# Four edits around the DeltaNet stages of a one-core hybrid block: one lane transpose for four, 22 weight low parts made in the feed-forward part, 128-row exponents, another stage order

## The chip, the cores and the metric

The kernel runs on one core of a Trainium2 chip. The metric is device time in microseconds (us); the median of the runs counts. A core has five engines that run on their own: TensorE (PE, matmuls; its weight loads are shown as PEld), VectorE (DVE), ScalarE (ACT), GpSimd (POOL) and SyncE (SP), which here issues every DMA. Each engine works through its own list of instructions in order; semaphores make one wait for another.

## What is computed

A block of two layers on 256 context and 256 latent tokens of width 1024. Layer 0 mixes tokens by a gated linear recurrence, layer 1 by a bidirectional gated DeltaNet with 8 key heads and 16 value heads of 128; behind each comes a SwiGLU feed-forward part of width 2816 (22 tiles of 128). Every sub-layer is normalised and modulated by six vectors that come from a product with `ada_w`. The DeltaNet of the reference, per chunk of tokens:

```
diff = gc[..., :, None] - gc[..., None, :]
decay = jnp.where(incl, jnp.exp(jnp.where(incl, diff, 0.0)), 0.0)
m = jnp.where(strict, jnp.einsum('bhid,bhjd->bhij', kb, kc) * decay, 0.0)
sol = lax.linalg.triangular_solve(m, rhs, left_side=True, lower=True, unit_diagonal=True)
u, w = sol[..., :d_v], sol[..., d_v:]
v_new = u - jnp.einsum('bhcd,bhde->bhce', w, s)
attn = jnp.where(incl, jnp.einsum('bhid,bhjd->bhij', qc, kc) * decay, 0.0)
```

All of it is float32.

## The kernel before

**Products.** A product of two float32 matrices is made from three fast matmuls (`mm3`, line 722): each operand is split into a high part, rounded to the short format `fp32r`, and a low part, the rest. For a weight tile of 128 x 1024 (`weight`, line 704) a DMA loads it as `raw`, ACT or DVE copies it to `whi`, and DVE or POOL subtracts (`wlo = raw - whi`). There are three raw buffers, and two each of `whi` and `wlo`. `product` (line 943) takes such a pair and issues 24 matmuls: 512 columns wide for keys and values and in the feed-forward part of layer 0, 256 wide for queries and the gate z.

**Background steps.** The feed-forward part of layer 0 (`ffn`, line 1099: 22 gate and up pairs, then the down products) also carries the modulation vectors of layer 1. `ada_later` queues generators, and every product takes one step of them by `bg_step`. A step (`ada_steps`, line 734) loads 128 x 1024 of `ada_w` into one of two buffers of the tile `ring`, multiplies it by a column of `cs` and adds to an accumulator.

**The DeltaNet stages.** Two key heads (four value heads) make a group; the groups are 0 to 3. The stages, each a function, are:

- A (line 1310), per key head: four products (k, two v, q), a convolution and SiLU (tile `cu`), transposes, and spills of k and v to device memory.
- E (line 1357), per group: the exponents of the decays. For each of eight pairs of chunk and direction `exponents` (line 1275) adds three matmuls in one bank: a column part (`pick` x `cT`, 64 rows deep, from `column`, line 1386), a row part (`rows` x `own`) and a mask (`below`, `identr`). ACT takes the exponential into the tile `gn`.
- N (line 1389), per group: `gn` is multiplied by the products of the keys (`ps_g`); then the 32 x 32 diagonal blocks of its 32 matrices are gathered into the tile `lw` by four DVE transposes of 32 partitions each, and inverted by 60 small DVE operations (`lmul`, `lw`). Two transposes of all 128 partitions (`ld`, `ldt`) bring them back.
- L (line 1432): the inverse is put together from the blocks by matmuls of 32 and of 64 rows (`ps_w`, `ps_z`) with copies between.
- P (line 1528): the exponents of the attention (`ps_a`, 16 groups of three matmuls; for one direction the column part is `npick` x `rT`, which is 128 rows deep) and their products with q.
- C (line 1552): the recurrence over the chunks (`ps_y`, `ps_s`, `ps_ks`, `ps_qs`, `ps_o`).
- Z and W: the gate products, and the first output products (`ps_wo`), which fill in.

**What sets the order.** Nothing is issued as written. A `Recorder` records all operations of a section and places them on the engines by priority: an operation's place in the program plus a bias of its stage. The string `PROG` sets in which order the stages are recorded, the table `TUNE['bias']` the biases, `_cost` what the planner takes an operation to last. Operations recorded through `R.copy`, `R.tt` and the like may go to either of two engines. Since all are issued by the planner, the profile puts them all down to line 612; they are told apart by the names of the tiles.

Of the kernel before, what the change touches and what calls it, by code (L numbers as in the profile page):

```python
# [21 lines left out]
NK = 8  # L22
EPS = 1e-6
FF = 22
NQK = 8
# [17 lines left out]
def _shuffle(sh, pattern, sizes):  # L43
# [18 lines left out]
    for g, n in zip(lhs, sh.shape, strict=True):  # L62
# [3 lines left out]
        for a in g:  # L66
# [5 lines left out]

PROG = "A0 A1 E0 A2 N0 A3 E1 L0 P0 N1 C0 A4 A5 E2 P1 L1 N2 C1 A6 Z0 A7 E3 L2 P2 N3 Z1 C2 Z2 Z3 L3 W0 P3 C3"
TUNE = dict(warm=5000, ev=3000, stay=(300, 0), g0=4, early=(1, 2, 4, 6), eb=0, ea=(0, 1, 1, 1), nwo=2, prog=PROG,
            bias={'C3': -1500, 'N0': 100, 'N': -700, 'Z3': -1200, 'L': -1500, 'E3': 700, 'W': 10000, 'L3': -800, 'E': -300, 'W0': 10000, 'P': -100, 'E0': -300, 'N3': -700, 'P2': 0, 'C': 400, 'A': 700, 'Z': 700, 'C1': 0})

# [122 lines left out]
class Recorder:  # L199
# [59 lines left out]
    def _cost(self, eng, method, out, ins, kw, args):  # L259
        n = out.free() if isinstance(out, _AP) else 1  # L260
        src_psum = any(i.t.psum for i in ins) or (isinstance(out, _AP) and out.t.psum)
        if eng == "PE":
            lhs, rhs = ins[0], ins[1]
            k, m, w = lhs.sh.shape[0], lhs.free(), rhs.free()
            if lhs.dt == F32R:
                return max(w / 2.4 + 13, 118)
            if method == "transpose":
                return 110 if k == 4 else 56
            if w <= 8:
                return 215  # L270
            if m <= 64:
                first = out.sh.flat[0] < out.t.sh.size // 4
                return (max(4 * w / 2.4, 54) + 2) if first or m > 32 else 27
            return max(4 * w / 2.4, 213) + 4
        if eng == "DVE":
            if method == "transpose":
                return 1.85 * n + 70
            if method == "tensor_tensor_scan":
                return 2.08 * n + 70
            if method == "reciprocal":  # L280
                return 6.4 * n + 60
            if method == "memset":
                return 0.3 * n + 40
            ptr = 65 if method in ("tensor_scalar", "scalar_tensor_tensor") and any(i.free() == 1 for i in ins) else 0
            one = method in ("tensor_scalar", "tensor_copy")
            return (0.52 if one and not src_psum else 1.04) * n + 65 + ptr
        if eng == "ACT":
            ptr = 65 * sum(1 for x in ("scale", "bias") if isinstance(kw.get(x), _AP))
            return 0.83 * max(n, ins[0].free()) + 95 + ptr
        if eng == "POOL":  # L290
            if method == "dma_start":
                return 1000
            if method == "affine_select":
                return 1.1 * n + 30
            if method == "memset":
                return 0.87 * n + 25
            if kw.get("op", args[3] if len(args) > 3 else None) == OP.pow:
                return 165 * n + 298
            return 2.25 * n + 30
        return 60  # L300
# [320 lines left out]
def hybrid_block(ctx: ExitStack, tc: tile.TileContext, I, out, dbg=None):  # L621
# [81 lines left out]

    def weight(*src, cols=1024, aside=False, place=None):

        r = raws.pop(0) if raws else raw_load(src, cols)
        hi, lo = place or (wp.tile([128, 1024], F32R, tag=t, bufs=NB[t], name=t) for t in ("whi", "wlo"))
        if aside:
            S.activation(hi[:, :cols], r[:, :cols], AF.Copy)
        else:  # L710
            R.copy(hi[:, :cols], r[:, :cols])
        (R.tt if (cur["wide"] or cur.get("flex")) and not aside else G.tensor_tensor)(lo[:, :cols], r[:, :cols], hi[:, :cols].bitcast(F32),
                                                                 OP.subtract)
        return hi, lo
# [19 lines left out]
    def ada_steps(l, m, direct=False):  # L734
# [35 lines left out]
        for t in range(2):  # L770
# [4 lines left out]
                        b.rearrange("p (g t o) -> p g t o", t=2, o=1).to_broadcast([128, 4, 2, 2]), OP.add)  # L775
        yield

    def ada_later(l, *ms, direct=False):
# [163 lines left out]

    def product(src, n_k, xs, n, wmap=lambda w, k: w[:, 128 * k:128 * k + 128]):
        wh, wl = early.pop(0) if early else weight(src)
        bg_step()
        ps = bank("mm", "ps_mm")
        for k in range(n_k):
            a, b = xs(k)
            mm3(ps[:, 0:n], wmap(wh, k), wmap(wl, k), a, b, k == 0, k == n_k - 1)
        return ps  # L950
# [148 lines left out]
    def ffn(l, n, upd, hh, hl, first=None):  # L1099
# [7 lines left out]
        for j in range(FF):  # L1107
# [3 lines left out]
            else:  # L1111
                pg = product(I["ffn_gu"][l, 0, j], NK, xk, n)
                pu = product(I["ffn_gu"][l, 1, j], NK, xk, n)
            sg = tmp(n, name="sg")
            S.activation(sg, pg[:, 0:n], AF.Silu)
# [15 lines left out]
    dump("x1", x.rearrange("p k t -> p (k t)"))  # L1131
    ada_later(1, 0, 1, 2, 3, 4, 5)

# [116 lines left out]
    V.tensor_scalar(npick, id64, -1.0, None, OP.mult)  # L1250
    pick = dn.tile([128, 32], F32R, name="pick")
    V.tensor_tensor(pick[0:64], ident[0:64, 0:32], ident[0:64, 32:64], OP.add)
    mod4 = piece(4)
# [21 lines left out]
    def exponents(g, c, d, sign, bound, col, to, name="ps_e"):  # L1275
# [3 lines left out]
        i = 4 * c + g  # L1279
        lhs, rhs, n = col  # L1280
        T.matmul(p4, lhs, rhs.rearrange("p (h o) -> p h o", o=1).to_broadcast([n, 4, 128]), start=True, stop=False, needs=to)
        T.matmul(p4, own[sign][:, i:i + 1].to_broadcast([128, 128]), rows[d], start=False, stop=False)
# [27 lines left out]
    def stage_a(h):  # L1310
        a = A[h] = {}

        ps = product(I["dn_w_in"][8 + h], NK, hx1, 512) if h else ps_k0
        kT = a["kT"] = dn.tile([128, 512], F32, tag="kT", bufs=8, name="kT")
# [17 lines left out]
        for j in range(2):  # L1332
            ps = product(I["dn_w_in"][16 + 2 * h + j], NK, hx1, 512)
            v2 = conv_silu(ps, 16 + 2 * h + j, 2)
# [22 lines left out]
    def stage_e(g):  # L1357
# [19 lines left out]
        T.transpose(pt[0:64, 0:128], cb.rearrange("p a s -> p (a s)").bitcast(F32), ident)  # L1377
        cT = t["cT"] = dn.tile([128, 128], F32R, tag="cT", bufs=2, name="cT")
        V.tensor_copy(cT[0:64], pt[0:64, 0:128])
# [6 lines left out]
    def column(t, c, d):  # L1386
        return t["cT"][0:64], pick[0:64, 4 * (2 * c + d):4 * (2 * c + d) + 4], 64

    def stage_n(g):
# [11 lines left out]
        for q in range(2):  # L1401
# [6 lines left out]
            for c in range(4):  # L1408
                for d in range(2):
                    e = g5[:, c, d, 2 * q:2 * q + 2, :]  # L1410
                    V.scalar_tensor_tensor(e, pg[:, 128 * c:128 * c + 128].rearrange("p (a i) -> p a i", a=1)
                                           .to_broadcast([128, 2, 128]), -1.0, e, OP.mult, OP.mult)

        w = dn.tile([128, 32, 32], F32, tag="lane", bufs=3, name="lw")
        for b in range(4):
            r = slice(32 * b, 32 * b + 32)
            V.transpose(w[r], gn[r, :, 32 * b:32 * b + 32].rearrange("p s f -> p f s"))
        V.memset(w.rearrange("p a b -> p (a b)")[:, 0:1024:33], 1.0)
# [109 lines left out]
    def stage_p(g):  # L1528
# [3 lines left out]
        for c in range(2):  # L1532
            for d in range(2):
                col = (rT[:, 1], npick[:, 16 * (2 + c) + 4 * g:16 * (2 + c) + 4 * g + 4], 128) if d else column(t, 2 + c, 0)
                p4 = exponents(g, 2 + c, d, 1, (1, -1)[d], col, t["at"], "ps_a")
# [298 lines left out]
```

## Time and profile before

| | us |
|---|---|
| median of three runs | 1360.35 |
| lowest and highest run | 1358.46, 1365.85 |
| profiled execution | 1364.68 |
| its span, first to last instruction | 1363.0 |

The mean granted clock of PE is 0.976 of the full one. Of the span, 262 to 610 us are the feed-forward part of layer 0, some 640 to 1130 the DeltaNet stages, and from 1157 on the feed-forward part of layer 1. In a row of a table by stage the busy time of an engine stands with the number of its instructions; a busy PE is not PE at its peak, since the ends of matmuls are modelled, and the distance from the start of one matmul to that of the next tells what one costs in a row. In rows of groups, `out<-in` are the names of the tiles, then count, busy us, mean ns, and the idle time before them with its releaser.

### The profile page before, as it was taken

How to read it: one execution, taken by the hardware profiler on the slowest of the kernel's cores; microseconds unless marked ns; L12 is line 12 of the kernel's file. 1: busy time of each engine (PE TensorE's matmuls, PEld its weight loads, DVE VectorE, ACT ScalarE, POOL GpSimd, SP SyncE). 2: the span in 40 equal slices, each digit the busy share in tenths (PEclk: the TensorE clock that was granted, in tenths of full speed). 3: DMA queues.
4: the chain of work that ended last, by engine and by line, in shares of the span. 5: the costliest groups of instructions: out<-in, count | busy, mean ns of one | idle time of the engine just before them, and what ended most of it. 6: DMA issues, size and time to landing. Idle time of an engine off the chain costs nothing.

```text
span 1363.0 us, 23260 instructions
## 1 busy us (share of the span) xinstructions
PE 1308.6 (96%) x9200; PEld 1110.3 (81%) x9200; DVE 1035.0 (76%) x1851; ACT 564.9 (41%) x1053; POOL 229.6 (17%) x203
## 2 busy tenths in 40 slices
PE   5999999899999999999998999999998998999997
PEld 3677778878888888888867788898798888999997
DVE  5799986988775665557868889798499376877775
ACT  3388773444321111005746656747646431211100
POOL 2000000110100001212524333334243100000000
PEclk9899999899999999999999999999999699999999
DMA  9545423365564665333523222323133025455563
GB/s 352 197 165 188 140 94 114 124 202 196 188 228 164 192 208 183 98 110 125 178 74 129 71 78 79 105 71 121 63 117 117 25 92 180 139 182 180 179 181 116
DMA packets 61261, 195.60 MB, mean 144 GB/s; under 512 B 6752, under 2 KB 9952, under 8 KB 60896
## 3 DMA queue, kind: packets, MB, share of 16 engines
q1 hardware_dynamic: 61152, 194.12, 42.8%
q8 instruction: 72, 1.18, 0.4%
q14 instruction: 37, 0.30, 0.1%
HBM read 184.13 MB, written 9.96 MB: 142 GB/s over the span
## 4 chain that ended last, share of the span: by engine, by line
PE 56%; issue 15%; DVE 6%; ACT 4%; DMA 1%; POOL 0%; POOLq 0%; SPq 0%; ACTq 0%; DVEq 0%
PE ps_mm L612 29%; PE ps_dn L612 9%; PE ps_e L612 2%; PE ps_wo L612 2%; PE ps_y L612 2%; PE ps_w L612 2%; PE ps_z L612 2%; PE ps_s L612 1%; DVE lw L612 1%; PE ps_ks L612 1%; DVE cu L612 1%; PE ps_a L612 1%; PE ps_qs L612 1%; PE ps_o L612 1%; ACT gn L612 1%
## 5 line engine op out<-in xcount | busy, mean ns | idle before, releaser
L612 PE MATMUL ps_mm<-hh,whi 128*128 128x512 f32 (+1 forms) x888 | 327.4, 370 | 8.0 <-DVE cu L612 5.6
L612 PE MATMUL ps_mm<-hl,whi 128*128 128x512 f32 (+1 forms) x888 | 327.3, 370 | 0.9 <-DVE hl L612 0.8
L612 PE MATMUL ps_mm<-hh,wlo 128*128 128x512 f32 (+1 forms) x888 | 326.2, 368 | 1.7 <-POOL wlo L612 1.7
L612 DVE TENSOR_TENSOR wlo<-raw,whi 128x1024 fp32r<-128x1024 f32 (+2 forms) x183 | 220.5, 1205 | 17.4 <-ACT whi L612 8.3
L612 DVE CAST whi<-raw 128x1024 fp32r<-128x1024 f32 (+2 forms) x177 | 120.2, 679 | 145.8 <-PE ps_mm L612 81.0
L612 POOL TENSOR_TENSOR wlo<-raw,whi 128x1024 fp32r<-128x1024 f32 x55 | 132.0, 2402 | 506.5 <-DVE whi L612 351.3
L612 PEld LDWEIGHTS ps_mm<-hh,whi 128*128 128x128 f32 x888 | 169.6, 191 | 40.6 <-issue 9.9
L612 PEld LDWEIGHTS ps_mm<-hh,wlo 128*128 128x128 f32 x888 | 169.7, 191 | 29.6 <-POOL wlo L612 2.4
L612 PEld LDWEIGHTS ps_mm<-hl,whi 128*128 128x128 f32 x888 | 170.0, 192 | 27.4 <-DVE hl L612 2.0
L612 PE MATMUL ps_dn<-fh,wlo 128*128 128x256 f32 (+1 forms) x374 | 122.7, 328 | 0.0
L612 PE MATMUL ps_dn<-fl,whi 128*128 128x256 f32 (+1 forms) x374 | 122.5, 327 | 0.0
L612 PE MATMUL ps_dn<-fh,whi 128*128 128x256 f32 (+1 forms) x374 | 122.2, 327 | 0.0
L612 PE MATMUL ps_mm<-h2h,whi 128*128 128x256 f32 x352 | 100.4, 286 | 1.1 <-ACT h2h L612 1.1
L612 PE MATMUL ps_mm<-h2l,whi 128*128 128x256 f32 x352 | 100.6, 286 | 0.5 <-DVE h2l L612 0.3
L612 PE MATMUL ps_mm<-h2h,wlo 128*128 128x256 f32 x352 | 100.1, 284 | 0.0
L612 ACT ACTIVATE whi<-raw 128x1024 fp32r<-128x1024 f32 (+2 forms) x61 | 63.2, 1036 | 77.8 <-PE ps_mm L612 45.1
L612 ACT ACTIVATE fh<-sg 128x256 fp32r<-128x256 f32 (+1 forms) x43 | 22.4, 522 | 156.4 <-DVE sg L612 156.3
L612 ACT ACT_TABLE_LOAD x59 | 75.7, 1283 | 7.0 <-DMA sm<-small 3.4
L612 PEld LDWEIGHTS ps_dn<-fl,whi 128*128 128x128 f32 x374 | 71.1, 190 | 6.4 <-issue 0.4
L612 PEld LDWEIGHTS ps_dn<-fh,wlo 128*128 128x128 f32 x374 | 71.1, 190 | 6.4 <-issue 0.4
L612 PEld LDWEIGHTS ps_dn<-fh,whi 128*128 128x128 f32 x374 | 71.1, 190 | 6.0
L612 DVE SCALAR_TENSOR_TENSOR x<-ring,cs,x 128x1024 f32<-128x1024 f32 x49 | 63.9, 1304 | 15.4 <-DMA ring<-ada_w 14.4
(326 smaller groups left out, 2544.7 us busy)
## 6 DMA issues: line engine op xcount, KB each, us to landing
ring<-ada_w SPq DMA_DIRECT2D x96, 512.0 KB, 4.5
raw<-ffn_gu SPq DMA_DIRECT2D x88, 512.0 KB, 3.5
raw<-dn_w_in SPq DMA_DIRECT2D x49, 512.0 KB, 3.5
raw<-ffn_down SPq DMA_DIRECT2D x34, 512.0 KB, 3.6
raw<-rg_w_in SPq DMA_DIRECT2D x16, 512.0 KB, 4.5
raw<-ffn_down SPq DMA_DIRECT2D x17, 384.0 KB, 3.4
raw<-dn_w_out SPq DMA_DIRECT2D x12, 512.0 KB, 3.6
raw<-rg_w_out SPq DMA_DIRECT2D x10, 512.0 KB, 3.4
```

Of the source, the lines that this page charges most:

```text
L612: call(*[real(x) for x in args], **{n: real(v) for n, v in kw.items()})
```

## The change

It has five parts.

1. In `exponents` the column part gets 128 rows: `cT` becomes two fixed tiles with zeros in rows 64 to 127, and `pick` is zero there.
2. In stage N, ACT copies the four diagonal blocks into a tile `lc`, and one DVE transpose of 128 partitions makes `lw`.
3. For 22 key and value weight tiles of stage A (all but that of the first key and of the first value) the low part is made in the feed-forward part of layer 0, as 22 further background steps: load into `ring`, copy on ACT, subtraction, store to device memory. Stage A then loads `wlo` by a DMA into its place. Every second pair of the feed-forward part takes one background step more.
4. `PROG` and the biases are others: A0 to A3 come first, E3 stands ahead of Z0 and L2, and P3 and L3 ahead of Z3.
5. The planner's costs of three kinds of operation are others; these change no instruction, only places.

```
-PROG = "A0 A1 E0 A2 N0 A3 E1 L0 P0 N1 C0 A4 A5 E2 P1 L1 N2 C1 A6 Z0 A7 E3 L2 P2 N3 Z1 C2 Z2 Z3 L3 W0 P3 C3"
+PROG = "A0 A1 A2 A3 E0 E1 N0 L0 P0 A4 N1 C0 P1 A5 E2 L1 N2 C1 A6 A7 E3 Z0 L2 P2 C2 Z1 N3 Z2 L3 P3 Z3 W0 C3"
...
-    def weight(*src, cols=1024, aside=False, place=None):
+    def weight(*src, cols=1024, aside=False, place=None, low=None):
...
+        if low is not None:
+            R.copy(hi, r)
+            sync.dma_start(out=lo.bitcast(F32), in_=low)
+            return hi, lo
...
+    def low_steps(tiles):
+
+        low = dr.tile([len(tiles), 128, 1024], F32, name="low")
+        for n, i in enumerate(tiles):
+            r, hi = next(cur["araw"]), cur["acc"][:, 1]
+            sync.dma_start(out=r, in_=I["dn_w_in"][i], after=cur["late"])
+            S.activation(hi.bitcast(F32R), r, AF.Copy)
+            R.tt(r.bitcast(F32R), r, hi, OP.subtract)
+            sync.dma_start(out=low[n], in_=r)
+            LOW[i] = low[n]
+            yield
...
+                bg_step(l == 0 and j % 2)
...
-    ada_later(1, 0, 1, 2, 3, 4, 5)
+    ada_later(1, 0, 1)
+    cur["bg"].append(low_steps([i for h in range(NQK) for i in (8 + h, 16 + 2 * h, 17 + 2 * h)][2:2 + TUNE["low"]]))
+    ada_later(1, 2, 3, 4, 5)
...
+    G.memset(pick.bitcast(F32), 0.0)
+    cTs = [dn.tile([128, 128], F32R, name=f"cT{i}") for i in range(2)]
+    for x in cTs:
+        G.memset(x[64:128].bitcast(F32), 0.0)
...
     def column(t, c, d):
-        return t["cT"][0:64], pick[0:64, 4 * (2 * c + d):4 * (2 * c + d) + 4], 64
+        return t["cT"], pick[:, 4 * (2 * c + d):4 * (2 * c + d) + 4]
...
+        lc = dn.tile([128, 32, 32], F32, tag="lane", bufs=3, name="lc")
         w = dn.tile([128, 32, 32], F32, tag="lane", bufs=3, name="lw")
         for b in range(4):
             r = slice(32 * b, 32 * b + 32)
-            V.transpose(w[r], gn[r, :, 32 * b:32 * b + 32].rearrange("p s f -> p f s"))
+            S.activation(lc[r], gn[r, :, 32 * b:32 * b + 32], AF.Copy)
+        V.transpose(w, lc.rearrange("p s f -> p f s"))
```

What the planner makes of it, at three places. On SP, in the feed-forward part of layer 0, near the last gate and up products: `raw` are that part's weights, `ring` the buffers of the background steps. Before:

```order
L612 DMA raw<-ffn_gu 128x1024
L612 DMA ring<-ada_w 128x1024 x2
L612 DMA raw<-ffn_gu 128x1024 x3
L612 DMA raw<-ffn_down 128x1024 x2
L612 DMA ring<-ada_w 128x1024 x2
L612 DMA raw<-ffn_down 128x768
```

And now:

```order
L612 DMA ring<-dn_w_in 128x1024
L612 DMA raw<-ffn_gu 128x1024
L612 DMA low<-ring 128x1024 x2
L612 DMA ring<-dn_w_in 128x1024
L612 DMA raw<-ffn_gu 128x1024
L612 DMA ring<-dn_w_in 128x1024
L612 DMA raw<-ffn_down 128x1024
L612 DMA low<-ring 128x1024 x2
```

Where pairs of ada loads stood between weight loads, two loads and two stores of low parts go round with two weight loads.

On SP at the start of the DeltaNet stages, with `wlo<-low` the low parts that come back. Before:

```order
L612 DMA raw<-dn_w_in 128x1024 x3
L612 DMA kspill<-k 128x512
L612 DMA raw<-dn_w_in 128x1024
L612 DMA kl<-kspill 128x512
L612 DMA raw<-dn_w_in 128x1024
```

And now:

```order
L612 DMA raw<-dn_w_in 128x1024
L612 DMA wlo<-low 128x1024
L612 DMA raw<-dn_w_in 128x1024 x3
L612 DMA kspill<-k 128x512
L612 DMA raw<-dn_w_in 128x1024
L612 DMA kl<-kspill 128x512
L612 DMA wlo<-low 128x1024
L612 DMA vspill<-vp 128x512
```

Each low part stands ahead of a weight load and waits for PE to have done with its buffer.

On DVE, around the lane transpose of group 3 (`gn` is the tile of the matrices, `lw` the gathered blocks, `lc` ACT's copy of them). Before:

```order
L612 SCALAR_TENSOR_TENSOR gn<-ps_g,gn 128x256 x16
L612 SCALAR_TENSOR_TENSOR r<-ps_ks,nbc,vl 128x128
L612 STREAM_TRANSPOSE lw<-gn 32x1024 x4
L612 SCALAR_TENSOR_TENSOR r<-ps_ks,nbc,vl 128x128
L612 MEMSET lw 128x32
L612 SCALAR_TENSOR_TENSOR r<-ps_ks,nbc,vb 128x128
```

And now:

```order
L612 COPY zs<-ps_mm 128x256
L612 CAST whi<-raw 128x1024
L612 TENSOR_TENSOR wlo<-raw,whi 128x1024
L612 TENSOR_TENSOR zs<-zs,onl 128x512
L612 STREAM_TRANSPOSE lw<-lc 128x1024
L612 MEMSET lw 128x32
L612 TENSOR_TENSOR wlo<-raw,whi 128x1024
```

The four transposes have become one. Before, stage C of group 2 stood around it (`r`); now the work of stage Z does.

More of the change, by code (lines that the diff above doesn't have):

```diff
@@ L70, in _shuffle @@
     return a.reshape([int(np.prod([dims[x] for x in g])) for g in rhs])
-PROG = "A0 A1 E0 A2 N0 A3 E1 L0 P0 N1 C0 A4 A5 E2 P1 L1 N2 C1 A6 Z0 A7 E3 L2 P2 N3 Z1 C2 Z2 Z3 L3 W0 P3 C3"
-TUNE = dict(warm=5000, ev=3000, stay=(300, 0), g0=4, early=(1, 2, 4, 6), eb=0, ea=(0, 1, 1, 1), nwo=2, prog=PROG,
-            bias={'C3': -1500, 'N0': 100, 'N': -700, 'Z3': -1200, 'L': -1500, 'E3': 700, 'W': 10000, 'L3': -800, 'E': -300, 'W0': 10000, 'P': -100, 'E0': -300, 'N3': -700, 'P2': 0, 'C': 400, 'A': 700, 'Z': 700, 'C1': 0})
+PROG = "A0 A1 A2 A3 E0 E1 N0 L0 P0 A4 N1 C0 P1 A5 E2 L1 N2 C1 A6 A7 E3 Z0 L2 P2 C2 Z1 N3 Z2 L3 P3 Z3 W0 C3"
+TUNE = dict(low=22, warm=5000, ev=3000, stay=(300, 0), g0=4, early=(1, 2, 4, 6), eb=0, ea=(0, 1, 1, 1), nwo=2, prog=PROG,
+            bias={'C3': -1200, 'N0': 100, 'N': -700, 'Z3': -1200, 'L': -1500, 'E3': 400, 'W': 10000, 'L3': -800, 'E': 400, 'W0': 10000, 'P': 600, 'E0': -300, 'N3': -700, 'P2': 0, 'C': 400, 'A': 1700, 'Z': 700, 'C1': 0, 'Z1': 400, 'A3': 1700, 'N2': -1000, 'L0': -800})
 class _Tile:
@@ L272, in _cost @@
                 first = out.sh.flat[0] < out.t.sh.size // 4
-                return (max(4 * w / 2.4, 54) + 2) if first or m > 32 else 27
+                return (max(4 * w / 2.4, 54) + (12 if m > 32 else 2)) if first or m > 32 else 27
             return max(4 * w / 2.4, 213) + 4
@@ L276, in _cost @@
             if method == "transpose":
-                return 1.85 * n + 70
+                return 1.92 * n + 75
             if method == "tensor_tensor_scan":
@@ L288, in _cost @@
             ptr = 65 * sum(1 for x in ("scale", "bias") if isinstance(kw.get(x), _AP))
-            return 0.83 * max(n, ins[0].free()) + 95 + ptr
+            return 0.83 * max(n, ins[0].free()) + 95 + ptr + (150 if "accum_out" in kw else 0)
         if eng == "POOL":
@@ L776, in ada_steps @@
         yield
+    LOW = {}
+    def low_steps(tiles):
[8 more added lines that the diff above has]
+            yield
     def ada_later(l, *ms, direct=False):
@@ L941, in hybrid_block, with product @@
     ol = m0.tile([128, NK, 512], F32R, name="ol", tag="ol", bufs=1)
-    def product(src, n_k, xs, n, wmap=lambda w, k: w[:, 128 * k:128 * k + 128]):
-        wh, wl = early.pop(0) if early else weight(src)
+    def product(src, n_k, xs, n, wmap=lambda w, k: w[:, 128 * k:128 * k + 128], low=None):
+        wh, wl = early.pop(0) if early else weight(src, low=low)
         bg_step()
@@ L1279, in exponents @@
         i = 4 * c + g
-        lhs, rhs, n = col
-        T.matmul(p4, lhs, rhs.rearrange("p (h o) -> p h o", o=1).to_broadcast([n, 4, 128]), start=True, stop=False, needs=to)
+        lhs, rhs = col
+        T.matmul(p4, lhs, rhs.rearrange("p (h o) -> p h o", o=1).to_broadcast([128, 4, 128]), start=True, stop=False, needs=to)
         T.matmul(p4, own[sign][:, i:i + 1].to_broadcast([128, 128]), rows[d], start=False, stop=False)
@@ L1311, in stage_a @@
         a = A[h] = {}
-        ps = product(I["dn_w_in"][8 + h], NK, hx1, 512) if h else ps_k0
+        ps = product(I["dn_w_in"][8 + h], NK, hx1, 512, low=LOW.get(8 + h)) if h else ps_k0
         kT = a["kT"] = dn.tile([128, 512], F32, tag="kT", bufs=8, name="kT")
@@ L1332, in stage_a @@
         for j in range(2):
-            ps = product(I["dn_w_in"][16 + 2 * h + j], NK, hx1, 512)
+            ps = product(I["dn_w_in"][16 + 2 * h + j], NK, hx1, 512, low=LOW.get(16 + 2 * h + j))
             v2 = conv_silu(ps, 16 + 2 * h + j, 2)
@@ L1377, in stage_e @@
         T.transpose(pt[0:64, 0:128], cb.rearrange("p a s -> p (a s)").bitcast(F32), ident)
[L1378 removed]
+        cT = t["cT"] = cTs[g % 2]
         V.tensor_copy(cT[0:64], pt[0:64, 0:128])
@@ L1533, in stage_p @@
             for d in range(2):
-                col = (rT[:, 1], npick[:, 16 * (2 + c) + 4 * g:16 * (2 + c) + 4 * g + 4], 128) if d else column(t, 2 + c, 0)
+                col = (rT[:, 1], npick[:, 16 * (2 + c) + 4 * g:16 * (2 + c) + 4 * g + 4]) if d else column(t, 2 + c, 0)
                 p4 = exponents(g, 2 + c, d, 1, (1, -1)[d], col, t["at"], "ps_a")
```

## The prediction

> **What bounds the kernel now.** I read the page first, then a table by stage, then the waits of TensorE (PE) at the places where the table shows it idle, and last the timeline of the steps that the change edits. The page's busy row and the row of granted clock:
>
> ```profile
> PE 1308.6 (96%) x9200; PEld 1110.3 (81%) x9200; DVE 1035.0 (76%) x1851; ACT 564.9 (41%) x1053; POOL 229.6 (17%) x203
> PEclk9899999899999999999999999999999699999999
> ```
>
> PE is busy in 96% of the span, so time comes off where PE's own work shrinks, where PE waits, or where its clock is halved. The table by stage (PE, PEld, DVE, ACT, POOL busy, then the clock, the DMA share and GB/s):
>
> ```profile
> 262.00:478.00 216.00, 216.00 (x993) 175.48 (x992) 159.75 (x166) 63.53 (x80) 14.81 (x6) 1.00 0.58 193
> 478.00:610.00 132.00, 132.00 (x621) 108.38 (x620) 75.49 (x88) 15.37 (x27) 16.82 (x7) 1.00 0.48 150
> 640.00:700.00 60.00, 59.77 (x299) 46.09 (x297) 40.98 (x110) 44.65 (x85) 24.25 (x13) 1.00 0.40 132
> 700.00:718.00 18.00, 13.30 (x71) 10.94 (x71) 17.64 (x24) 6.75 (x9) 7.28 (x4) 1.00 0.27 88
> 762.00:796.00 34.00, 34.00 (x542) 28.29 (x541) 30.73 (x50) 23.96 (x53) 13.00 (x9) 1.00 0.28 87
> 1000.00:1040.00 40.00, 39.75 (x293) 37.21 (x292) 38.28 (x108) 21.92 (x53) 10.61 (x11) 1.00 0.37 122
> 1040.00:1053.00 13.00, 9.46 (x70) 8.39 (x68) 12.92 (x30) 6.07 (x10) 4.29 (x4) 1.00 0.38 130
> 1053.00:1077.00 24.00, 22.80 (x441) 20.97 (x441) 6.89 (x10) 13.03 (x28) 4.25 (x5) 0.50 0.13 42
> ```
>
> The first feed-forward part (262 to 610) is wholly PE's: DVE is at 74% and 57% there. In the DeltaNet part PE is full too, but in two stretches DVE is the one that is full while PE stands: 700 to 718 (PE 13.30 of 18, DVE 17.64) and 1040 to 1053 (9.46 of 13, DVE 12.92). Both lie inside a lane stage N: that of head group 0 and that of group 3, whose result stage L needs. Behind the second one the clock is 0.50 for 24 us, in which the 32- and 64-row matmuls of L3 run. What PE waited for in the two places:
>
> ```profile
> PE ps_mm L612 <- DVE cu L612: 4.8, 2, 3.1
> PE ps_wo L612 <- POOL ol L612: 3.2, 2, 2.2
> ```
>
> **128 rows in the exponents.** Stage E issues 32 groups of three matmuls (pick, rows, below), stage P 8 more of this kind. Only the first of the three has 64 rows. Five rows of stage E of group 0, then four of a group in stage P whose first matmul (npick) has 128 rows already:
>
> ```profile
> 686.99 0.39 PE L612 MATMUL ps_mm<-hh,whi 128*128 128x512 f32 x1
> 687.31 0.48 PE L612 MATMUL ps_e<-pick,cT 64*128 64x512 f32 x1
> 687.72 0.50 PE L612 MATMUL ps_e<-rows,own 128*128 128x512 f32 x1
> 688.06 0.40 PE L612 MATMUL ps_e<-below,identr 128*128 128x512 f32 x1
> 688.39 0.48 PE L612 MATMUL ps_e<-pick,cT 64*128 64x512 f32 x1
> ```
>
> ```profile
> 1023.69 0.38 PE L612 MATMUL ps_a<-npick,rT 128*128 128x512 f32 x1
> 1023.90 0.40 PE L612 MATMUL ps_a<-rows,own 128*128 128x512 f32 x1
> 1024.14 0.40 PE L612 MATMUL ps_a<-identr,below 128*128 128x512 f32 x1
> 1024.37 0.38 PE L612 MATMUL ps_a<-npick,rT 128*128 128x512 f32 x1
> ```
>
> By starts, the group with 64 rows takes 1.08 us (688.39 - 687.31), the one with 128 rows 0.68. The difference is paid at the switches: 0.32 into pick from 686.99, 0.41 and 0.34 behind it, against 0.21 to 0.24. So the edit is worth 0.40 us a group.
>
> ```profile
> L612 PE MATMUL ps_e<-pick,cT 64*128 64x512 f32 x32 | 14.3, 467 | 0.0
> L612 PE MATMUL ps_a<-pick,cT 64*128 64x512 f32 x8 | 3.8, 480 | 0.0
> ACT gn L612 <- PE ps_e L612: 13.7, 19, 2.3
> ```
>
> 40 groups make 16.0 us. A few of them share a switch (two picks in a row), and it counts in full only where PE is the bound; 640 to 700 holds stage E of group 0 with PE at 59.77 of 60, and ACT, which takes the groups up, waits 13.7 us for PE and not the other way round. I take -14, with -8 and -16 as ends. The Trainium skill, "TensorEngine Tiling (Array Packing)", section "When to Use Tiling", speaks against the edit: a contraction of 64 should be kept for two-fold row tiling, so that two tiles share the array. By that rule the edit would gain nothing (0 in place of -14); the rows above show 64 rows dearer here, since nothing runs in the other half.
>
> **One lane transpose.** Stage N gathers four diagonal blocks by four DVE transposes of 32 partitions; the trace has one of 128 partitions in the same stage:
>
> ```profile
> 986.94 5.38 DVE L612 SCALAR_TENSOR_TENSOR gn<-ps_g,gn 128x256 f32<-128x256 f32 x16
> 992.50 8.22 DVE L612 STREAM_TRANSPOSE lw<-gn 32x1024 f32<-32x1024 f32 x4
> 1051.44 1.98 DVE L612 STREAM_TRANSPOSE ld<-lw 128x1024 f32<-128x1024 f32 x1
> L612 ACT ACTIVATE whi<-raw 128x1024 fp32r<-128x1024 f32 (+2 forms) x61 | 63.2, 1036 | 77.8 <-PE ps_mm L612 45.1
> L612 ACT ACT_TABLE_LOAD x59 | 75.7, 1283 | 7.0 <-DMA sm<-small 3.4
> ```
>
> DVE gets 8.22 - 1.98 = 6.2 us less in each of four groups, 25 us in all. ACT gets 16 copies of 1024 elements; the nearest row is 1.04 us, so 17 us, and by the built order 5 more table loads of 1.28 us. ACT is at 21.92 of 40 where DVE is fullest, so this is covered; without the cover the chain would still be no longer (4 x 1.04 + 1.98 = 6.1 us against 8.22). N3 started at 986.94 and gave its result only behind the 1.98 us from 1051.44, since DVE served it among other work. The two idle stretches of PE, 4.70 and 3.54 us, are 8.2 us; with DVE 6.2 lighter ahead of each, and with N3's products now ahead of L2 in PE's order, I take -6 (0 to -8.2). Late next is then the ACT copy into stage L.
>
> The 24 us at half clock: group 0's L stage stands in 762 to 796 at full clock, with products among its small matmuls. If L3's stretch ran at full clock, half of what PE does there would go, at most 22.80 / 2 = 11.4. L3 in the new order has as little between its small matmuls as before (4 products from the first of them to the first of stage C, 9 before), so I take -5, with 0 and -11 as ends.
>
> **22 low parts made early.** In the DeltaNet part the low part of a weight was a subtraction; now ACT, DVE and SP prepare it in the feed-forward part, and a DMA brings it back.
>
> ```profile
> L612 DVE TENSOR_TENSOR wlo<-raw,whi 128x1024 fp32r<-128x1024 f32 (+2 forms) x183 | 220.5, 1205 | 17.4 <-ACT whi L612 8.3
> L612 POOL TENSOR_TENSOR wlo<-raw,whi 128x1024 fp32r<-128x1024 f32 x55 | 132.0, 2402 | 506.5 <-DVE whi L612 351.3
> L612 PE MATMUL ps_mm<-hh,wlo 128*128 128x512 f32 (+1 forms) x888 | 326.2, 368 | 1.7 <-POOL wlo L612 1.7
> ring<-ada_w SPq DMA_DIRECT2D x54, 512.0 KB, 4.4
> raw<-dn_w_in SPq DMA_DIRECT2D x49, 512.0 KB, 3.5
> kspill<-k SPq DMA_DIRECT2D x8, 256.0 KB, 2.5
> x2d<-x SPq DMA_DIRECT2D x1, 1024.0 KB, 3.8
> ```
>
> By the built order POOL loses 25 of these (60 us of an engine that is 17% busy) and DVE none: worth nothing by itself, apart from the 1.7 us that PE waits for POOL. What it adds comes in two places. In the feed-forward part DVE takes 22 x 1.2 = 27 us more in 348 us in which it was busy 235; PE covers that. But SP, one queue in order, now goes round in turns of two loads, two weight loads and two stores, and the next load waits until the store of its buffer has landed. A turn is a load (4.4), the ACT copy (1.04), the DVE subtraction (1.2) and the store (between 2.5 and 3.8, say 3.2): 9.8 us. PE uses two weights a turn, 48 matmuls of 0.22 us (216.00 us for 993 in the table), 10.6 us. So it fits by 0.8 us, and three raw buffers give a cushion; queued behind a late store are PE's weights. I take +2, ends 0 and +12. In the DeltaNet part a low part arrives 3.5 us after its buffer is freed where POOL took 2.4. The product before it takes 24 x 0.22 = 5.3 us and hides that; behind a 256-column product (half as long, seven times) about 0.8 us shows: +2 of a bound of 0 to +6 (SP's raw loads and spills queue behind the same wait).
>
> **Other order.** A0 to A3 come first, E3 and N3 ahead of L2. Nothing in the trace prices it. It shifts where DVE is full: groups 2 and 3 now share DVE with L2 and C2. I take +2, with -6 and +10 as ends.
>
> **Sum.** -14 - 6 - 5 + 2 + 2 + 2 = -19 us. The profiled execution took 1364.7 us for its span of 1363.0, 4.3 above the median of the three timed runs (1360.35); I take the 19 us off the median: 1341 us. A difference under 0.5% (6.8 us) can't be told from none.
>
> **Rivals.**
> - Clock kept (1330 us, 0.15). PE no longer stands before L3, so the clock stays up: -11 in place of -5, DVE's waits go whole (-8) and the order gives -1 and not +2: -30. For it: the 0.50 stretch begins right behind the idle one. Against it: L3 is still sparse. The Trainium skill, "TensorE: Matmul & The Clock Gate", section "What's actually happening", says that the clock halves after an idle window of some 3.4 us; by that rule no wait here (longest 2.2 us) would have halved it, but the trace shows 0.50, so I don't lean on it.
> - Gain given back (1355 us, 0.20). PE's 14 us come back as waits for DVE, since DVE was at 38.28 of 40 in 1000 to 1040 and the new order packs N3 beside L2: -14 + 9 = -5, with the other terms taken up in it.
> - SP's turns too long (1374 us, 0.07). With six transfers in a turn the landings grow; the loads into ring have landed after 3.3 to 10.8 us in this trace:
>
> ```profile
> DMA to landing us min/median/max: 3.3/4.5/10.8
> ```
>
>   Each microsecond of a turn over 10.6 costs PE 11 us in 11 turns, less the cushion, by my estimate 9 (two weights of 5.3 us held ready, less what the pair being loaded has used up). It decides from a turn of 11.4 on; at 14.6 it is 44 - 9 = +35 against -21 for the rest: +14.
> - That an edit doesn't take place can be left out: the built order shows no 64-row pick, no fourfold transpose and 22 loads of low parts.
>
> **How the numbers follow.** The forecast itself has 0.58, from 1331 to 1350. Faster by over 0.5% are the forecast, the kept clock and a part of the given-back case: 0.78. Within 0.5%: 0.14, nearly all of it given back. Slower: 0.08. From 1326 to 1358 leaves out the slow rival, the worse third of the given-back case and the better third of the kept clock, under 0.2 together.
>
> **What would show it.** Right: pick rows with 128 rows and groups of about 0.68 us; four transposes of some 2.0 us in place of 16; PE full in the feed-forward part; POOL near 170 us busy; some 35 MB more DMA (66 transfers of 512 KB); less idle PE ahead of L0 and L3. Wrong: PE under 0.97 of the feed-forward part with waits for weights behind SP, PE waits for a wlo DMA in the DeltaNet part, or idle PE in stage N or L of group 2 of over 8 us.

## The result and the profile after

The changed kernel takes 1353.2 us (median of 8 runs, 1347.3 to 1355.6); the kernel before took 1360.7 in 8 runs beside it (1358.5 to 1368.3), 7.5 us more. The ratio, which goes by the means (1352.5 and 1362.7), is 0.9925 with a 95% interval of 0.9897 to 0.9954: 10 us faster, between 6 and 14. The forecast was 19 us faster. The profiled execution took 1349.2 us, at the lower end of its runs, and that of before 1364.7, near its upper end, so the two traces differ by 15.5 us. What follows splits those 15.5 us, and they overstate the change by some 5.

A part of that excess goes with the clock. Every run comes with the mean granted clock of its span. In the changed kernel's eight runs it is 0.973 to 0.982, mean 0.978, and the profiled run has the highest of the eight. In 63 runs of the kernel before, timed beside the experiments, it is 0.974 to 0.983, mean 0.978 too, and 0.976 in the profiled one. So over all runs the change took nothing off what the clock costs, although the two traces differ there.

The page of the changed kernel, its row of busy time and that of granted clock:

```profile
PE 1294.4 (96%) x9200; PEld 1112.0 (83%) x9200; DVE 1043.8 (77%) x1879; ACT 605.8 (45%) x1085; POOL 163.9 (12%) x177
PEclk9999999899999999999999999999999799999998
```

PE is 14 us less busy and still in 96% of the span; POOL is 66 us less busy. The table by stage (columns as in the prediction):

```profile
262.00:478.00 216.00, 213.40 (x973) 173.18 (x972) 163.84 (x167) 78.43 (x94) 15.94 (x6) 1.00 0.70 239
478.00:610.00 132.00, 128.48 (x577) 104.34 (x576) 89.45 (x100) 24.02 (x35) 7.21 (x3) 0.99 0.73 241
700.00:718.00 18.00, 17.85 (x95) 14.93 (x93) 15.21 (x31) 13.65 (x25) 3.02 (x2) 1.00 0.26 85
1000.00:1040.00 40.00, 38.49 (x296) 37.00 (x296) 38.23 (x101) 23.78 (x53) 9.76 (x9) 1.00 0.36 118
1040.00:1064.00 24.00, 20.50 (x434) 19.00 (x434) 10.12 (x15) 16.40 (x32) 7.15 (x10) 0.57 0.11 35
```

Two things have turned round. The feed-forward part, where PE never stood, now has idle PE (2.60 and 3.52 us in the first two rows). And ahead of stage L of group 0, where PE was busy for 13.30 of 18 us, it is now busy for 17.85 (group 0's transposes into `lw` begin at 714.3 us in place of 704.9, and PE has no idle stretch of over 1 us from 650 to 835 us). The clock still falls to half over stage L of group 3 (20.5 us of it, 23.9 before).

From the groups of the changed kernel: the one transpose, ACT's copies ahead of it, and the low parts still left to POOL (55 before):

```profile
L612 DVE STREAM_TRANSPOSE lw<-lc 128x1024 f32<-128x1024 f32 x4 | 8.2, 2052 | 5.0 <-PE ps_z L612 4.6 <-ACT lc L612 0.4
L612 ACT ACTIVATE lc<-gn 32x1024 f32<-32x1024 f32 x16 | 16.9, 1055 | 3.7 <-DVE gn L612 3.5
L612 POOL TENSOR_TENSOR wlo<-raw,whi 128x1024 fp32r<-128x1024 f32 x30 | 74.1, 2471 | 592.9 <-DVE whi L612 457.8 <-ACT whi L612 67.1 <-issue 22.1
```

**The feed-forward part lost 8.7 us.** Its first `sg` product on DVE and its last down matmul on PE, before:

```profile
L612 DVE TENSOR_TENSOR sg<-sg,ps_mm x22: 679/680/687, 262.4 to 499.0; 128x512 f32<-128x512 f32 x22
L612 PE MATMUL ps_dn<-fh,wlo x198: 281/389/499, 498.2 to 622.0; 128*128 128x512 f32 x154, 128*128 128x256 f32 x44
```

and after:

```profile
L612 DVE TENSOR_TENSOR sg<-sg,ps_mm x22: 674/680/689, 260.6 to 497.5; 128x512 f32<-128x512 f32 x22
L612 PE MATMUL ps_dn<-fh,wlo x198: 278/389/774, 497.4 to 628.8; 128*128 128x512 f32 x154, 128*128 128x256 f32 x44
```

From the start of the one to the start of the other it is 359.5 us before and 368.3 after. The waits of PE in that part say for what:

```profile
PE ps_ada L612 <- DVE x L612: 6.1, 3, 2.6
```

PE did not wait for weights there. It waited three times for DVE to finish the sum `x` of a modulation vector, so that PE could select its result (`ps_ada`); a half-clock stretch of 3.4 us follows the second wait. The first of the three, 2.6 us at 371.9 us, is not there in the traces of e5, e6 and e7 below, whose lists for this part are those of the changed kernel (in this order):

```profile
PE ps_ada L612 <- DVE x L612: 2.9, 2, 1.7
PE ps_ada L612 <- DVE x L612: 3.9, 3, 2.3
PE ps_ada L612 <- DVE x L612: 3.0, 2, 2.4
```

The part is 363.8, 366.0 and 365.4 us long there. So the same lists lose 4 to 9 us from run to run, and this trace shows the most; without low parts (before, e1, e2, e3, e9) the part is 359.3 to 359.5 us in every trace. The reason for the second wait is in the timeline of those sums, all in the changed kernel's trace:

```profile
507.88 1.28 DVE L612 SCALAR_TENSOR_TENSOR x<-ring,cs,x 128x1024 f32<-128x1024 f32 x1 [1.55 <-DMA ring<-ada_w]
511.02 1.28 DVE L612 SCALAR_TENSOR_TENSOR x<-ring,cs,x 128x1024 f32<-128x1024 f32 x1
513.42 1.28 DVE L612 SCALAR_TENSOR_TENSOR x<-ring,cs,x 128x1024 f32<-128x1024 f32 x1 [1.13 <-DMA ring<-ada_w]
517.10 1.28 DVE L612 SCALAR_TENSOR_TENSOR x<-ring,cs,x 128x1024 f32<-128x1024 f32 x1 [0.36 <-DMA ring<-ada_w]
519.16 1.28 DVE L612 SCALAR_TENSOR_TENSOR x<-ring,cs,x 128x1024 f32<-128x1024 f32 x1 [0.77 <-DMA ring<-ada_w]
520.59 0.64 PE L612 MATMUL ps_ada<-x,sel 128*32 128x256 f32 x8 [2.65 <-DVE x L612]
```

A step of the sum comes every 2.8 us ((519.16 - 507.88) / 4) and waits for its load nearly every time: a load into `ring` takes 4.5 us to land and DVE 1.28 to use it, so two buffers give a step every (4.5 + 1.28) / 2 = 2.9 us. The sums run as fast as two buffers allow: they are late, and behind the low parts on SP. The first and the last pair of stores that issue on SP:

```profile
381.36 2.68 SPq L612 DMA_DIRECT2D low<-ring  x2
...
490.21 3.43 SPq L612 DMA_DIRECT2D low<-ring  x2
```

Ten turns of two low parts took 108.85 us, 10.9 a turn. That is PE's pace of two weights, and PE lost nothing there; but with the extra background step the program asks for two and a half steps in that time, and SP did two.

**The DeltaNet part gained 21.7 us.** From the last down matmul to the last output product, before and after, with the same number of matmuls:

```profile
621.95:1152.49 530.54, 508.09 (x4569) 437.97 (x4568) 418.45 (x979) 298.57 (x634) 171.10 (x145) 0.97 0.30 99
```

```profile
628.84:1137.65 508.81, 489.90 (x4568) 437.34 (x4567) 401.21 (x985) 311.61 (x639) 111.45 (x122) 0.98 0.37 126
```

With 1.9 us from an earlier start of the feed-forward part (the instructions ahead of it are the same, and that start scatters from 258.1 to 264.9 us in the fourteen traces) and 0.6 behind the last output product, the ledger is -1.9 + 8.7 - 21.7 - 0.6 = -15.5.

### The profile page after: what moved, and what is told of

It is laid out like the page before. It is cut to its first block, busy times and chain, and to the rows that moved or that the text cites. A ratio compares the mean times of both kernels' runs of the same rounds, so it can differ in the third digit from the quotient of the medians.

```text
span 1347.5 us, 23452 instructions
## 1 busy us (share of the span) xinstructions
PE 1294.4 (96%) x9200; PEld 1112.0 (83%) x9200; DVE 1043.8 (77%) x1879; ACT 605.8 (45%) x1085; POOL 163.9 (12%) x177
## 4 chain that ended last, share of the span: by engine, by line
PE 52%; issue 16%; DVE 6%; ACT 4%; DMA 3%; POOL 1%; POOLq 0%; DVEq 0%; SPq 0%; ACTq 0%
PE ps_mm L612 28%; PE ps_dn L612 7%; DMA ring<-ada_w 2%; PE ps_y L612 2%; PE ps_wo L612 2%; PE ps_z L612 2%; PE ps_w L612 2%; PE ps_s L612 2%; DVE x L612 2%; PE ps_e L612 1%; PE ps_ks L612 1%; PE ps_qs L612 1%; PE ps_o L612 1%; ACT L612 1%; ACT gn L612 1%
## 5 line engine op out<-in xcount | busy, mean ns | idle before, releaser
L612 DVE CAST whi<-raw 128x1024 fp32r<-128x1024 f32 (+1 forms) x174 | 119.2, 685 | 147.2 <-PE ps_mm L612 98.7
L612 PEld LDWEIGHTS ps_mm<-hl,whi 128*128 128x128 f32 x888 | 169.0, 191 | 27.9 <-issue 2.5
L612 POOL TENSOR_TENSOR wlo<-raw,whi 128x1024 fp32r<-128x1024 f32 (+1 forms) x32 | 76.6, 2396 | 601.9 <-DVE whi L612 457.8
```

Of the source, the lines that this page charges most:

```text
L612: call(*[real(x) for x in args], **{n: real(v) for n, v in kw.items()})
```

## The experiments

Every kernel was timed beside the kernel before. One ledger serves for all of them. In the DeltaNet part I took from each trace the time that the exponents' matmuls hold PE (from the start of a `ps_e` or `ps_a` matmul to the start of the next matmul), PE's idle time, and the time at half clock, by the clock's records, of which half counts as lost. What then remains is the rest of PE's work. The last column is the mean granted clock of the whole span, over all runs and in the one that was traced:

| kernel | ratio to before | DeltaNet part | exponents | idle PE | at half clock | rest | clock, runs / trace |
|---|---|---|---|---|---|---|---|
| before | 1 | 530.5 | 44.6 | 22.5 | 34.1 | 446.4 | 0.978 / 0.976 |
| changed | 0.9925 | 508.8 | 33.5 | 18.9 | 23.9 | 444.4 | 0.978 / 0.982 |
| e1 rows only | 1.0004 | 529.4 | 33.9 | 31.2 | 44.4 | 442.1 | 0.974 / 0.976 |
| e2 lane only | 1.0097 | 538.7 | 45.3 | 26.5 | 41.0 | 446.4 | 0.977 / 0.977 |
| e9 order only | 1.0114 | 545.7 | 45.0 | 31.6 | 54.6 | 441.9 | 0.972 / 0.972 |
| e10 low only | 1.0116 | 537.8 | 45.0 | 28.3 | 37.5 | 445.7 | 0.975 / 0.977 |
| e5 changed, 64 rows | 1.0023 | 531.0 | 46.2 | 19.8 | 41.0 | 444.5 | 0.978 / 0.975 |
| e6 changed, 4 transposes | 1.0138 | 543.7 | 33.5 | 40.4 | 58.0 | 440.8 | 0.971 / 0.971 |
| e7 changed, low on POOL | 1.0086 | 535.5 | 36.2 | 38.4 | 34.1 | 443.9 | 0.978 / 0.975 |
| e3 changed, no low | 1.0106 | 544.0 | 36.3 | 32.7 | 64.9 | 442.6 | 0.966 / 0.967 |
| e8 changed, old order | 1.0035 | 527.9 | 33.8 | 27.9 | 41.0 | 445.8 | 0.978 / 0.971 |
| e11 changed, old costs | 1.0016 | 527.7 | 35.8 | 27.8 | 44.4 | 441.9 | 0.974 / 0.972 |
| e4 changed, select later | 0.9910 | 509.3 | 33.5 | 18.8 | 23.9 | 445.0 | 0.979 / 0.977 |
| e12 changed, select latest | 0.9985 | 519.0 | 33.5 | 21.7 | 41.0 | 443.3 | 0.977 / 0.973 |

The rest is 441 to 446 us in all fourteen. So the length of this part is, within some 3 us, 444 us plus the exponents plus PE's idle time plus half of the time at half clock. A line fitted through the fourteen rows gives 0.40 us for a microsecond at half clock, not quite the half. The intervals of the ratios are about 0.002 to 0.003 to either side.

The times in a row are of one execution. By the last column the kernel before, the changed kernel, e4, e5, e7, e8 and e12 share one clock (0.977 to 0.979 over their runs), so what their traces differ by at half clock, 24 to 41 us, is of the single execution and not shown to be the kernel's. In every run of e3 and e6 the clock is lower than in any run of the kernel before, and in e9 it is 0.975 at most: there the loss is the kernel's own.

**e1, the 128-row exponents alone.** On the kernel before:

```
-        return t["cT"][0:64], pick[0:64, 4 * (2 * c + d):4 * (2 * c + d) + 4], 64
+        return t["cT"], pick[:, 4 * (2 * c + d):4 * (2 * c + d) + 4]
```

> The kernel before with the 128-row exponents alone. My theory: 40 groups fall from 1.08 to about 0.70 us, and PE's time from the end of the first feed-forward part to the last output product falls by 10 to 12 us; the total by 8 to 13 us (ratio 0.991 to 0.994). First rival, the gain comes back as waits for DVE: groups as short, but the DeltaNet part only 2 to 5 us shorter (ratio 0.997 or more). Second rival, by the skill's rule for 64 rows: groups as long as before, no change.

The exponents take 33.9 us instead of 44.6, so the 10.7 us are real, and the second rival is wrong. The Trainium skill, "TensorEngine Tiling (Array Packing)", section "When to Use Tiling", names two-fold row tiling for a contraction of 64; no run here tiles two such matmuls, so that is not tested. What the runs show is that a 64-row matmul alone among 128-row ones costs more than one filled up with rows of zeros. But nothing is left of the gain: ratio 1.0004 (0.9985 to 1.0024). The first rival is right. Idle PE grows by 8.7 us and half of the added half-clock time is 5.1; its runs have a lower clock too (0.974 against 0.978). PE's waits in its DeltaNet part, the three largest:

```profile
PE ps_mm L612 <- DVE cu L612: 7.5, 7, 2.5
PE ps_ks L612 <- DVE S L612: 3.8, 1, 3.8
PE ps_mm L612 <- POOL wlo L612: 3.1, 3, 1.1
```

PE got ahead and stood behind DVE and POOL.

**e2, the lane transpose alone.** On the kernel before, stage N as in the change:

```
-            V.transpose(w[r], gn[r, :, 32 * b:32 * b + 32].rearrange("p s f -> p f s"))
+            S.activation(lc[r], gn[r, :, 32 * b:32 * b + 32], AF.Copy)
+        V.transpose(w, lc.rearrange("p s f -> p f s"))
```

> The kernel before with the single lane transpose alone. My theory: DVE is 25 us less busy, PE's two waits ahead of the stages L of group 0 and of group 3 shrink, total 2 to 6 us less (ratio 0.995 to 0.999). Rival, DVE's load there was not what PE waited for (the chain of 60 small lane operations was): total within 1 us of before (ratio 0.999 to 1.001), idle PE in the DeltaNet part unchanged at some 25 us.

Both were wrong: 1.0097 (1.0074 to 1.0119), slower. The transposes into `lw` take 8.2 us instead of 32, but the planner lays out the whole part anew when one duration changes: it gave other operations to DVE, whose busy time in the part is 414 us against 418 before, and its order has 4 us more idle PE and 7 us more at half clock.

**e9, the stage order alone,** `PROG` and the biases of the change on the kernel before:

> The kernel before with the stage order and biases of the changed kernel alone. Theory one, a stage order is only worth something for the durations that it was laid out for: slower than before by 5 us or more (ratio 1.004 or more), the DeltaNet part 535 us or more. Rival, the order is better in itself (its absence cost 15 us in the changed kernel): faster by 5 us or more (ratio 0.996 or less).

Theory one holds: 1.0114 (1.0086 to 1.0143), with 9 us more idle PE and 20 more at half clock.

**e10, the low parts alone,** part 3 of the change on the kernel before:

> The kernel before with the 22 low parts made early and the extra background step alone. Theory one: POOL falls to some 110 us busy in the DeltaNet part, small operations of DVE no longer stand behind POOL's subtractions (the longest lmul well under 2.2 us), the DeltaNet part 5 to 12 us shorter than 530.5, the feed-forward part 4 to 8 us longer, total within 6 us of before (ratio 0.995 to 1.002). Rival, the low parts carry the change by themselves: ratio 0.993 or less.

Neither: 1.0116 (1.0087 to 1.0144). POOL is down to 119 us and the longest `lmul` to 1.1, as expected, but idle PE is up by 5.8, the half clock by 3.4, and the feed-forward part is 5 us longer; by the traces the kernel is 11 us longer and not 16, since the trace of before is of a run 4 us above its median.

The four parts alone thus make +0.5, +13, +15.5 and +16 us (the planner's costs alone were not tried). Together they make -10. So the next three undo one part each and keep the order: the planner is given the changed kernel's operations, and only what is put out in their places differs, so that each engine's list stays the changed kernel's.

**e5, 64 rows in the changed order:**

```
+                 emit=(lambda f, o, l, r, **k: f(o, l[0:64], r[0:64], **k)) if len(col) == 3 else None)
```

> The changed kernel in exactly its own order on every engine, but the column part of the 40 groups has 64 rows again. Theory one, the exponents' time is PE's own and the order of the changed kernel cashes it: groups back at about 1.05 us, DeltaNet part (508.8 us in the changed kernel, from the last down product to the last output product) 10 to 14 us longer, ratio to before 1.000 to 1.003. Rival, DVE stands behind PE and takes the gain back, as when the rows were changed alone: DeltaNet part 0 to 4 us longer, ratio 0.9925 to 0.996.

Theory one holds: 1.0023 (1.0001 to 1.0044), 13 us over the changed kernel. The exponents are 12.7 us longer, 0.32 a group. Idle PE hardly moves (0.9 us). In the trace the time at half clock is 17 us longer, half of which makes up the part's 22 us; over the runs the clock is the same as the changed kernel's (0.978), so that half is of this execution, and the 13 us of the timed runs are about what the exponents take. In this order the 128 rows pay in full; in the order of before they paid nothing.

**e6, four transposes in the changed order:**

```
+                    emit=lambda f, o, i: [f(o[32 * b:32 * b + 32], i[32 * b:32 * b + 32]) for b in range(4)])
```

> The changed kernel in exactly its own order, but the one lane transpose is issued as four of 32 partitions (ACT's copies stay). My theory: DVE 25 us busier, each chain of stage N 6 us later, PE's waits in the DeltaNet part (18.9 us idle) up by 4 to 10 us, ratio to before 0.996 to 1.000. Rival, the chain has slack in this order: DeltaNet part within 2 us of 508.8, ratio 0.991 to 0.994.

The direction of my theory, far beyond its size: 1.0138 (1.0107 to 1.0169), 29 us. Idle PE doubles, and the clock is lower in all its runs. Its largest waits in the DeltaNet part:

```profile
PE ps_mm L612 <- DVE cu L612: 7.6, 3, 6.3
PE ps_y L612 <- DVE r L612: 6.4, 2, 5.4
```

Neither is a wait for the lanes. PE's four longest idle stretches behind the boundary begin at 714.4, 806.3, 917.9 and 1012.0 us, and DVE begins the four transposes of a group at 710.5, 797.4, 911.6 and 1002.4: what PE waits for (`cu`, `S`, `r`) is work of other stages that is queued behind them on DVE, and four transposes take some 6 us more than one.

**e7, low parts by POOL in the changed order.** The low parts are still made and stored early, but not read; POOL subtracts where the load stood:

```
-            sync.dma_start(out=lo.bitcast(F32), in_=low)
+                    nc.gpsimd.tensor_tensor(got["lo"], got["r"], got["hi"].bitcast(F32), OP.subtract)
```

> The changed kernel in its own order, low parts still made in the feed-forward part, but in stage A the 22 low parts are subtracted by POOL at the place of the load, as most were before, and not loaded. Theory one, the early low parts carry the gain of the DeltaNet part: it gets 15 us or more longer (without them, in another order, it was 544.0 instead of 508.8), ratio 1.003 or more. Rival, what was lost without them is the order that the planner then finds: DeltaNet part 0 to 6 us longer, ratio 0.9925 to 0.997.

Theory one holds: 1.0086 (1.0054 to 1.0117), 22 us, about what idle PE (38.4 us, 19.5 more) and the exponents (2.7 more) make. DVE's list is the same, and yet DVE is 23 us busier in this part (424.12 against 401.21). The row of its lane products, in the changed kernel and then in e7 (ns: shortest, median, longest):

```profile
L612 DVE TENSOR_TENSOR lmul<-lw x120: 176/356/937, 718.9 to 1036.9; 128x30 f32<-128x30 f32 x8, 128x58 f32<-128x58 f32 x8, 128x84 f32<-128x84 f32 x8, 128x108 f32<-128x108 f32 x8
```

```profile
L612 DVE TENSOR_TENSOR lmul<-lw x120: 174/354/2407, 720.6 to 1059.2; 128x30 f32<-128x30 f32 x8, 128x58 f32<-128x58 f32 x8, 128x84 f32<-128x84 f32 x8, 128x108 f32<-128x108 f32 x8
```

The timeline of e7 at the longest:

```profile
764.30 2.39 POOL L713 TENSOR_TENSOR wlo<-raw,whi 128x1024 fp32r<-128x1024 f32 x1 [10.06 <-PE ps_e L612]
764.33 2.41 DVE L612 TENSOR_TENSOR lmul<-lw 128x30 f32<-128x30 f32 x1
```

An operation of 30 elements, 0.174 us at its shortest, lasts as long as POOL's subtraction beside it. The Trainium skill, "SBUF — State Buffer", section "Who interferes with whom", says that DVE and GpSimd share a port pair under an exclusive lock; this trace agrees (2.41 beside 2.39). The 240 lane operations (`lmul` and `lw`) sum to 96.6 us here and to 83.0 in the changed kernel, 13.6 of the 23 us; most of the others are again small operations.

**e3, no low parts, order left to the planner.** `low_steps` and the extra background step are taken out of the changed kernel:

> The changed kernel without the low parts and without the extra background step; low parts are subtracted in the DeltaNet part as before. My theory: the first feed-forward part is back at 367 us (374 in the changed kernel), the DeltaNet part is no longer than in the changed kernel by more than 2 us, so 4 to 7 us faster than the changed kernel: 1346 to 1349 us (ratio to before 0.989 to 0.992). Rival, the low parts made early carry the gain in the DeltaNet part by taking work off DVE and POOL: the feed-forward part is back at 367 but the DeltaNet part 7 us or more longer, and the total 1353 us or more (ratio 0.9945 or more).

The rival is right: 1.0106 (1.0084 to 1.0128). The feed-forward part is back at 359.3 us, but the DeltaNet part is 35 us longer, 14 by idle PE and 20 by the half clock, which is lower in all five runs (0.963 to 0.967).

**e8, old stage order.** `PROG` and the biases of before in the changed kernel:

> The changed kernel with the stage order and the biases of before; rows, lane transpose, low parts and the planner's costs stay. Theory one, the stage order carries the gain: DeltaNet part 525 us or more, ratio 1.003 or more (the feed-forward part keeps its 7 us). Rival, the other parts carry it: DeltaNet part 505 to 515 us, ratio 0.989 to 0.996.

Theory one: 1.0035 (1.0009 to 1.0060), 15 us over the changed kernel.

**e11, the planner's old costs.** The instructions are those of the changed kernel, in other places, some forty of them on another of DVE, ACT and POOL, where the program leaves that to the planner:

```
-                return 1.92 * n + 75
+                return 1.85 * n + 70
```

> The changed kernel with the planner's three costs of before; every instruction is the same, only places differ. My theory: another order of the same work is worth as much as a part of the change, so the time moves by 5 to 20 us, up rather than down (ratio to before 0.997 to 1.008). Rival, places matter little where the work is the same: within 4 us of the changed kernel (ratio 0.9895 to 0.9955).

My theory holds: 1.0016 (0.9994 to 1.0039), 12 us over the changed kernel by the planner's choice alone. Its DeltaNet part:

```profile
622.70:1150.40 527.70, 499.93 (x4568) 445.03 (x4567) 403.19 (x993) 311.80 (x637) 106.54 (x120) 0.96 0.36 122
```

DVE (403 us), ACT and POOL are as busy as in the changed kernel, and PE has 27.8 us idle instead of 18.9 and 44.4 us at half clock instead of 23.9. The gain of 10 us is no larger than what the planner's places move by themselves.

**e4 and e12, the selecting matmuls later.** To mend the feed-forward part, PE's selecting matmuls got a bias of 80 places, then of 150:

```
+            R.bias += 80
             for v in range(nv):
```

> The changed kernel, with PE's eight selecting matmuls that end each modulation vector placed some 30 to 55 rows later in PE's list. My theory, PE stands in the first feed-forward part only because these come ahead of DVE's accumulation: the three waits (6.1 us) go, the feed-forward part is 367 to 369 us long instead of 374, total 4 to 7 us less than the changed kernel (ratio to before 0.987 to 0.990). Rival, SP's turns with the stores are too long and PE would wait for them anyhow: the waits come back as waits for weights (whi, wlo) or at the later place, the feed-forward part stays at 373 us or more and the ratio at 0.992 or more.

> The changed kernel with PE's selecting matmuls of the modulation vectors placed some 55 to 115 rows later, all five of the feed-forward part. My theory, PE stands there only for DVE's accumulation: no wait over 1 us of ps_ada left, the feed-forward part 366 to 368 us long from 255.1 us (373.8 in the changed kernel), total 1344 to 1349 us (ratio 0.986 to 0.990). Rival, the next wait there is late too (weights behind SP's stores), or the DeltaNet part starts no earlier: feed-forward part 371 us or more, ratio 0.991 or more.

The waits of PE for DVE's sums in the feed-forward part, e4 and then e12:

```profile
PE ps_ada L612 <- DVE x L612: 2.1, 1, 2.1
```

```profile
PE ps_ada L612 <- DVE x L612: 5.2, 2, 3.9
```

In e4 two of the three waits are gone, and that part is 365.9 us instead of 368.3. That is no more than e5, e6 and e7 show with the selects in their old places (2.9 to 3.9 us of waits, 363.8 to 366.0 us), so the later place is not shown to do anything. The ratio is 0.9910 (0.9886 to 0.9933), below the changed kernel's 0.9925 by less than either interval: a better version is not shown either. In e12 the select that had stood at 520.6 us stands at 534.6 and waits again, by the code because one accumulator serves all vectors, so that the next sum starts only behind the select and the chain moves with it. The part is 372.1 us long, the rest of the order changed with it, and the ratio is 0.9985 (0.9966 to 1.0004), 8 us over the changed kernel. So a later place for the selects does not mend it. What e3 shows is that without the low parts and the extra step the waits are gone; which of the two it takes was not tried, nor were more buffers.

## Why the prediction was right, and where its terms were off

By direction and range it was right; the gain is about half of the 19 us. The 1353.2 us lie outside the forecast's own 1331 to 1350 and within 2 us of the rival "gain given back" (1355). What that rival said did not happen: it had 9 us coming back as waits for DVE in the DeltaNet part, and idle PE there fell by 3.6. Most of what is missing is the term of the half clock and what the feed-forward part lost; the first two terms fell short by 2 to 3 us each. Term by term, against the two traces and, where they bear on it, the other runs:

- **128 rows, -14.** 11.1 us off the exponents, 12.7 where the rows alone were undone. The mechanism is right, its size 0.28 to 0.32 us a group and not 0.40: the group that I read took 1.08 us, but all 32 of stage E took 31.2 us before, 0.98 each, and 22.5 after, 0.70 each. That it goes straight through to the end was wrong as a general claim: e1 gave all of it back. That 64 rows are dearer because nothing runs in the other half is not shown; the rows show where the time goes, to the changes between 64 and 128 rows.
- **DVE's stalls, -6.** Idle PE in the DeltaNet part fell by 3.6. The stall before L0 went from 4.70 to 0.15 us; around L3, 5.0 us of PE's idle time stand in the last two rows of the table by stage, as much as in the last three of before (0.25, 3.54 and 1.20).
- **Half clock, -5.** 34.1 us at half clock became 23.9, half of the difference is -5.1. That looks like the forecast, but it is the luck of the two traced runs: over all runs both kernels have a clock of 0.978, so the term is not borne out. Nor is the place right: L3's stretch shrank only from 23.9 to 20.5 (20.5 in e4, e5, e7 and e12 too), and two short ones (at 718 and at 1131 us) went.
- **Low parts in the feed-forward part, +2.** This is the step that failed: 8.7 in this trace, 4.3 to 6.5 in three others with the same lists. I had estimated SP's turn (9.8, measured 10.9) and asked only whether weights would be late. They were not. PE also takes the modulation sums from the same queue and buffers, and those were.
- **Low parts in the DeltaNet part, +2,** and POOL's relief worth nothing. For such a load PE waited once:

```profile
PE ps_mm L612 <- DMA wlo<-low: 0.7, 1, 0.7
```

  The relief is not nothing in the new order: e7 puts it at 22 us in that order. In the order of before POOL cost DVE's lanes little (83.5 us for the 240 operations, and 80.0 in e10, which takes the same work off POOL), which is why that trace did not show it.
- **Order, +2 with -6 to +10.** Too narrow. The order decides over as much as the largest of the other terms: 12 us between e11 and the changed kernel with the same instructions, 15 by the stage order (e8 and e9).

The deeper fault is that the sum treated idle PE and half clock as belonging to edits. Idle PE belongs to the order, and the half clock to the order and to the single run: idle plus half of the half-clock time is 31 us in the changed kernel's trace, 40 before, and 40 to 69 in all others but e4. With the clock of all runs in place of the trace's (one less the clock, times the span) it is 49 us, 53 before, and 50 to 81 in all others but e4 (47). So the change gained 11.1 us by the exponents, 3.6 by idle PE and 2.0 in the rest, with no worse a clock, and lost 4 to 9 in the feed-forward part: 8 to 12 us, where the timed runs say 10. Each part alone had more idle PE (26 to 32 us against 22.5). The forecast came out on the right side because the changed kernel's order could be read, and its two known stalls had other work in them; it did not follow from the prices of the parts.

What stays open: e5 to e7 hold an order that was laid out for the shorter durations, so their 13, 29 and 22 us may be more than a part is worth in an order laid out without it; what sets the clock over stage L of group 3 is not known; and whether some order of the kernel before would do as well was not tried.

## What to carry to other kernels

Where a planner lays out the whole program, test an edit twice: replanned, and with the order held and only the instruction swapped. Here the two differ in sign for the lane transpose and the low parts (e2 and e10 against e6 and e7, though on different kernels), and a replanned result carried 12 us of the planner's own. Split the time of the bound engine into its work, its idle time and its clock before explaining any of it: here PE's work apart from the exponents was 441 to 446 us in fourteen kernels, and what else differed was idle time and clock. One trace gives the clock of one execution: compare it with the clock of all runs before putting it down to an edit. When work is moved under a busy engine, list everything which that engine takes from the queue it is moved to, not only the largest stream.

## What the hardware showed beyond that

- A DVE operation with two inputs lasted as long as the POOL subtraction that ran beside it (2.41 us, against 0.174 for the shortest of that kind). In e7, 22 subtractions of 2.4 us on an engine that is busy for 164 of 536 us went along with 23 us more on DVE.
- The clock fell to half over stage L of group 3 in every one of these kernels, for 14 to 31 us, although no wait of PE from 1040 us on was longer than this one in the changed kernel:

```profile
PE ps_w L612 <- DVE at L612: 2.0, 1, 2.0
```

  The same 32- and 64-row matmuls ran at full clock in stages L of groups 0 to 2, in the traces of the kernel before and of the changed one; in group 0 of before products stand among them (762 to 796 us). Whether it is the missing products that let the clock fall was not tested.
